# Attention in an encoder layer: row normalisation on VectorE, reciprocals for two rows at once, value tiles of two heads, the two output parts summed by a DMA, and another order of loads ahead of the up-projection

## The chip, the cores and the metric

The program runs on one core of one Trainium2 chip. A core has five engines with a queue each: TensorE (PE in the profile; its weight loads are PEld), VectorE (DVE), ScalarE (ACT), GpSimd (POOL) and SyncE (SP), which here only issues DMAs. Each engine works through its own queue in order and waits at semaphores for the others. The time is the device time of one execution in microseconds: before the change 1638.55 us, the median of three runs (1635.51 to 1639.82).

## The reference

One encoder layer on x of 1024 positions by 1024 channels, in float32 throughout. Cut to what matters here:

```python
h = layer_norm(x) * (1 + sc1) + sh1
proj = h @ w_in                    # q, k, v of 2 x 8 heads of 64, forget logits, two gates
# branch A, "fox": causal softmax attention, bias F[t] - F[s]
# branch B, "chunk": each block of 128 queries sees at most 5 key blocks, bias by distance
p = softmax(logits + bias)         # per head and query row
o = p @ v                          # 64 columns per head
merged = sigmoid(gate_a) * (o_a @ w_br_fox) + sigmoid(gate_c) * (o_c @ w_br_chunk)
x = layer_norm(alpha * x + (1 + g1) * (merged @ w_out), ln1_g, ln1_b)
u = causal_depthwise_conv(h2 @ w_up)                 # 1024 -> 2 x 2816
x = layer_norm(alpha * x + (1 + g2) * ((silu(a) * val) @ w_down), ln2_g, ln2_b)
```

## The kernel before

Every product is made of float32r operands that are split in a high part (a cast, on ACT) and a low part (the difference, on POOL or DVE), and summed as high*high + high*low + low*high. A weight that is loaded from memory passes `split` (L97 to L103): ACT casts `wh`, POOL subtracts `wl`; only then its buffer `ws` is free for the next load on SP. There are two `ws` buffers.

The attention loop (L678 to L717) takes eight pairs of heads, the chunk pairs 4 to 7 first, then the fox pairs 2, 3, 0, 1. Each head goes through four steps `g`; a step takes two blocks of 128 query rows, here called row 0 and row 1 of the step. While step n is finished, step n+1 is begun:

- `scores` (L429): two matmuls per piece of keys into `pss`, on DVE the bias and the row minimum (L460; `mx`), on ACT the exponential with the row sum `sm` (L466), on DVE its reciprocal `rc` (L468), and a multiplication of the row by `rc`: on ACT for row 0 if it has over 512 keys (L470), on POOL else (L472). In fox, POOL first prepares the diagonal piece of the bias, `fm` (L453).
- `probs` (L485): PE transposes the row in pieces of 128 keys (L501), ACT casts (L505), DVE subtracts (L506).
- `weighted` (L509): the transposed rows against the value tile `vs` of the head (L516). Its columns are the 64 high parts and the 64 low parts of the values, so the 128 rows of the result are two parts of the output that have to be added: ACT copies one half across (L520, `ot`), DVE adds (L521) into `o32`, a tile that two heads fill; one store to `od` per pair and half (L708).

Between these stand matmuls of the "stream" (projections of later heads, values, gates: L216 to L218, L312 to L314), which fill PE. A list scheduler puts the instructions of all engines in the order in which they are issued, by its own estimates, so a change at one place can move rows elsewhere.

After the attention come the branch products, the output product and the first normalisation, then the up-projection: for eight of the 22 blocks of columns (`c < HEAD`) in a form with prepared sums that `wd` holds, for the others from `w_up` directly. Blocks are taken in the order 0, 8, 1, 9, ... (L223). Weights wait in two buffers `fs` and two buffers `ws`. Of block 0, all four prepared parts are loaded early into `fs` (L992); `head` (L808) multiplies parts of blocks 0 to 7 ahead of the loop, with the two `ws`. The loop (L1146) lets the second half of a block alternate with the first half of the next; the eviction L1062 (`add`) reads a product that a later product of the block goes on summing in.

Of the kernel before, what the change touches and what calls it, by code (L numbers as in the profile page):

```python
# [11 lines left out]
F32 = mybir.dt.float32  # L12
# [6 lines left out]
P = 128  # L19
# [23 lines left out]
def body(ctx, tc, a, out):  # L43
# [256 lines left out]
    def unit_v(br, grp):  # L300
        n = 264 if (br, grp) == (1, 0) else 256

        def run(ws):
            tiles = [ap0.tile([P, NT, P], F32R, name=nm("vs"), tag="vs", bufs=6) for _ in range(4)]
            v_now[br, grp] = tiles
            for t in range(NT):
# [8 lines left out]
                for i in range(4):  # L315
                    src = ps[:, i * DH : (i + 1) * DH]
                    se.copy(out=tiles[i][:, t, 0:DH], in_=src)
                    ve.tensor_sub(out=tiles[i][:, t, DH:P], in0=src, in1=tiles[i][:, t, 0:DH])
# [110 lines left out]
    def scores(hd, g, i):  # L429
# [35 lines left out]
        sm = small.tile([P, 1], F32, name=nm("sm"), tag="sm")  # L465
        se.activation(out=st[:, 0:nk], in_=st[:, 0:nk], func=AF.Exp, scale=-1.0, bias=prev, accum_out=sm)  # L466
        rc = small.tile([P, 1], F32, name=nm("rc"), tag="rc")
        ve.reciprocal(out=rc, in_=sm)  # L468
        if nk > 512 and not i:
            se.mul(out=st[:, 0:nk], in_=st[:, 0:nk], mul=rc)  # L470
        else:
            po.tensor_scalar_mul(st[:, 0:nk], st[:, 0:nk], rc)  # L472
        return st
# [35 lines left out]
    def weighted(hd, g, which, pt, o32):  # L509
        br, h = hd[4], hd[5]  # L510
        vs = v_now[br, h // 4][h % 4]
        j0, nj = pv_span(br, g)
        ps = pso.tile([P, H], F32, name=nm("pso"), tag="o")
        for j in range(nj):
            for c in range(2):
                pe.matmul(ps[:, 0:256], vs[:, j0 + j, :], pt[c][j // 4][:, j % 4, :], start=j == 0 and c == 0,  # L516
                          stop=j == nj - 1 and c == 1)
        own, other = slice(which * DH, (which + 1) * DH), slice((1 - which) * DH, (2 - which) * DH)
        tmp = ap.tile([P, 256], F32, name=nm("ot"), tag="ot", bufs=1)
        se.copy(out=tmp[own, :], in_=ps[other, 0:256])  # L520
        ve.tensor_tensor(out=o32[own, g % 2 * 256 : (g % 2 + 1) * 256], in0=ps[own, 0:256], in1=tmp[own, :], op=ALU.add)  # L521
# [138 lines left out]
    o_now = {}  # L660
# [12 lines left out]
    sts = {(0, i): scores(heads[steps[0][:2]], 0, i) for i in range(2)}  # L673
# [4 lines left out]
    for u, (ip, _) in enumerate(plan):  # L678
# [5 lines left out]
        for n in range(8 * u, 8 * u + 8):  # L684
# [3 lines left out]
            for qt in range(2):  # L688
                if n + 1 < len(steps):
# [5 lines left out]
                    sts[n + 1, qt] = scores(heads[nip, ni], ng, qt)  # L695
                probs(hd, g, qt, sts.pop((n, qt)), pt)
                passed += 0.5 * cost_of(n)
                while stream.cur < upto and spent * main < passed * fill:
                    spent += stream.step()
                    ticks += 1  # L700
                    if ticks % 2 or next(beside, aside) is aside:
                        next(aside, None)
            if g % 2 == 0:
                if i == 0:
# [13 lines left out]
    for _ in chain(beside, aside):  # L718
        pass
# [645 lines left out]
```

## Time and profile before

| | before |
|---|---|
| median of three runs | 1638.55 us (1635.51 to 1639.82) |
| profiled execution, its own time | 1642.11 us |
| its span | 1640.3 us |
| PE busy | 1533.1 us (93%) |
| DVE, ACT, POOL busy | 1132.2, 819.2, 595.9 us |
| mean granted clock of PE | 0.977 |

Busy time is that in which an engine works; the matmuls overlap, so a busy PE is not PE at its peak. A wait in brackets behind an instruction is the time that the engine stood idle before it, with the writer that ended it. The median us from issue to landing of a DMA include its queueing.

### The profile page before, as it was taken

How to read it: one execution, taken by the hardware profiler on the slowest of the kernel's cores; microseconds unless marked ns; L12 is line 12 of the kernel's file. 1: busy time of each engine (PE TensorE's matmuls, PEld its weight loads, DVE VectorE, ACT ScalarE, POOL GpSimd, SP SyncE). 2: the span in 40 equal slices, each digit the busy share in tenths (PEclk: the TensorE clock that was granted, in tenths of full speed). 3: DMA queues.
4: the chain of work that ended last, by engine and by line, in shares of the span. 5: the costliest groups of instructions: out<-in, count | busy, mean ns of one | idle time of the engine just before them, and what ended most of it. 6: DMA issues, size and time to landing. Idle time of an engine off the chain costs nothing. (4 is left out here: it accounts for less than half of the span.)

```text
span 1640.3 us, 22725 instructions
## 1 busy us (share of the span) xinstructions
PE 1533.1 (93%) x7689; PEld 1280.5 (78%) x7689; DVE 1132.2 (69%) x2309; ACT 819.2 (50%) x1473; POOL 595.9 (36%) x579
## 2 busy tenths in 40 slices
PE   6898999989998999999898896999999999999996
PEld 3787788778887988887787675788888888888885
DVE  6738787687656555444759878477778776756688
ACT  3546555554554555664323536444454544456451
POOL 1124344343643454543106354544445454000000
PEclk9999999999999999999999897999999999999999
DMA  9035786776444133334644634533453222597552
GB/s 365 26 95 165 244 260 219 245 227 210 163 122 146 49 109 97 106 97 163 230 141 170 228 117 142 191 135 116 148 179 122 97 96 91 203 380 243 187 192 78
DMA packets 117957, 270.62 MB, mean 165 GB/s; under 512 B 12368, under 2 KB 21136, under 8 KB 117840
## 3 DMA queue, kind: packets, MB, share of 16 engines
q1 hardware_dynamic: 112560, 260.16, 47.9%
q10 hardware_dynamic: 4752, 7.17, 1.2%
q0 software_dynamic: 528, 1.84, 0.3%
q8 instruction: 61, 1.00, 0.2%
q14 instruction: 56, 0.46, 0.1%
HBM read 193.32 MB, written 67.40 MB: 159 GB/s over the span
## 5 line engine op out<-in xcount | busy, mean ns | idle before, releaser
L102 POOL TENSOR_TENSOR wl<-ws,wh 128x1024 fp32r<-128x1024 f32 x54 | 132.7, 2461 | 229.0 <-ACT wh L101 229.0
L472 POOL TENSOR_SCALAR s<-s,rc 128x128 f32<-128x128 f32 (+3 forms) x96 | 146.7, 1529 | 139.3 <-DVE rc L468 108.5
L792 PE MATMUL psu<-hc,wx 128*128 128x512 f32 x720 | 168.4, 389 | 0.0
L792 PEld LDWEIGHTS psu<-hc,wx 128*128 128x128 f32 x720 | 135.1, 188 | 28.1
L1030 DVE SCALAR_TENSOR_TENSOR pcv<-u,convp,pcv 128x1024 f32<-128x1024 f32 x88 | 113.2, 1286 | 45.6 <-ACT pcv L1028 44.6
L1171 DVE TENSOR_TENSOR op<-rw,op 128x512 fp32r<-128x512 f32 x146 | 93.5, 687 | 52.7 <-ACT op L1170 52.4
L466 ACT ACTIVATE s<-s,mx 128x640 f32<-128x640 f32 (+7 forms) x128 | 94.5, 739 | 69.3 <-DVE mx L460 68.2
L1170 ACT CAST op<-rw 128x512 fp32r<-128x512 f32 x146 | 85.2, 622 | 83.2 <-PE psd L1183 41.4
L505 ACT CAST pt<-pst 128x512 fp32r<-128x512 f32 (+1 forms) x192 | 82.0, 451 | 76.8 <-PE pst L501 73.3
L1182 PE MATMUL psd<-op,op 128*128 128x512 f32 x292 | 113.7, 389 | 0.9 <-DVE op L1171 0.9
L1181 PE MATMUL psd<-op,op 128*128 128x512 f32 x292 | 113.6, 389 | 0.0
L1183 PE MATMUL psd<-op,op 128*128 128x512 f32 x292 | 113.6, 389 | 0.0
L216 PE MATMUL psq<-h1h,wh 128*128 128x512 f32 x256 | 105.6, 414 | 0.0
L506 DVE TENSOR_TENSOR pt<-pst,pt 128x512 fp32r<-128x512 f32 (+1 forms) x192 | 96.4, 518 | 11.8 <-ACT pt L505 10.1
L216 PE MATMUL psg<-h1h,wh 128*128 128x512 f32 x256 | 103.9, 406 | 0.0
L217 PE MATMUL psq<-h1l,wh 128*128 128x512 f32 x256 | 102.1, 399 | 1.2 <-DVE h1l L213 1.2
L218 PE MATMUL psq<-h1h,wl 128*128 128x512 f32 x256 | 101.9, 398 | 0.8 <-POOL wl L102 0.8
L501 PE MATMUL pst<-ident,s 128*128 128x128 f32 x528 | 82.6, 276 | 19.5 <-POOL s L472 16.7
L218 PE MATMUL psg<-h1h,wl 128*128 128x512 f32 x256 | 100.2, 391 | 0.0
L217 PE MATMUL psg<-h1l,wh 128*128 128x512 f32 x256 | 100.1, 391 | 0.0
L516 PE MATMUL pso<-pt,vs 128*128 128x256 f32 x608 | 93.1, 291 | 3.6 <-DVE pt L506 3.1
L516 PEld LDWEIGHTS pso<-pt,vs 128*128 128x128 f32 x608 | 83.3, 194 | 12.7 <-DVE pt L506 4.9
(267 smaller groups left out, 4025.3 us busy)
## 6 DMA issues: line engine op xcount, KB each, us to landing
ws<-in_w_up SPq DMA_DIRECT2D x36, 512.0 KB, 3.4
wa<-in_w_ada SPq DMA_DIRECT2D x64, 256.0 KB, 3.4
dr<-in_w_down SPq DMA_DIRECT2D x22, 512.0 KB, 4.9
rw<-td SPq DMA_DIRECT2D x44, 256.0 KB, 4.6
yd<-y SPq DMA_DIRECT2D x20, 512.0 KB, 2.7
rw<-yd SPq DMA_DIRECT2D x40, 256.0 KB, 4.1
rw<-sd SPq DMA_DIRECT2D x33, 256.0 KB, 4.6
wa<-in_w_ada SPq DMA_DIRECT2D x8, 1024.0 KB, 10.7
```

The costliest lines, as they stand in the source:

```text
L102: po.tensor_sub(out=lo, in0=st, in1=hi)
L216: pe.matmul(ps, wh, xh, start=start, stop=False)
L217: pe.matmul(ps, wh, xl, start=False, stop=False)
L218: pe.matmul(ps, wl, xh, start=False, stop=stop)
L472: po.tensor_scalar_mul(st[:, 0:nk], st[:, 0:nk], rc)
L506: ve.tensor_sub(out=dl, in0=src, in1=dh)
L516: pe.matmul(ps[:, 0:256], vs[:, j0 + j, :], pt[c][j // 4][:, j % 4, :], start=j == 0 and c == 0, stop=j == nj - 1 and c == 1)
L792: pe.matmul(ps, w[:, a_, k, :], h[k][b_], start=first, stop=k == 3 and a_ == 1, skip_group_check=on)
L1030: ve.scalar_tensor_tensor(out=ps, in0=u[b][:, 2 - d : S + 2 - d], scalar=cp[:, 2 - d : 3 - d], in1=ps, op0=ALU.mult, op1=ALU.add)
L1181: pe.matmul(ps[t], g[:, 0, ts], d[:, 0], start=start, stop=False, skip_group_check=on)
L1182: pe.matmul(ps[t], g[:, 0, ts], d[:, 1], start=False, stop=False, skip_group_check=on)
L1183: pe.matmul(ps[t], g[:, 1, ts], d[:, 0], start=False, stop=stop, skip_group_check=on)
```

## The change

1. The sums of a step's two rows go into one tile of two columns; `normed` takes both reciprocals in one DVE instruction, after both exponentials, and multiplies each row: row 0 of over 512 keys on ACT as before, every other row on DVE. POOL has no part in it any more.
2. A value tile holds two heads (three buffers of two heads each in place of six of one), so the evictions of the values take two heads at a time: 64 casts and 64 subtractions in place of 128 each.
3. `weighted` ends with one ACT copy of all 128 rows into `o32`, which now belongs to one head; there is no addition on DVE. SP stores rows 0 to 63 of it to `od`; one step later POOL issues a DMA that adds rows 64 to 127 to the same place. That is 32 stores on SP in place of 16, and 32 DMAs on POOL.
4. Ahead of the up-projection, the two `fs` buffers take block 0's first two parts and the second half of the weights of block 8; block 0's other two parts go through `ws`.

```diff
...
-            tiles = [ap0.tile([P, NT, P], F32R, name=nm("vs"), tag="vs", bufs=6) for _ in range(4)]
+            tiles = [ap0.tile([P, 2, NT, P], F32R, name=nm("vs"), tag="vs", bufs=3) for _ in range(2)]
...
-                for i in range(4):
-                    src = ps[:, i * DH : (i + 1) * DH]
-                    se.copy(out=tiles[i][:, t, 0:DH], in_=src)
-                    ve.tensor_sub(out=tiles[i][:, t, DH:P], in0=src, in1=tiles[i][:, t, 0:DH])
+                for i in range(2):
+                    src = ps[:, i * P : (i + 1) * P].rearrange("p (h d) -> p h d", h=2)
+                    se.copy(out=tiles[i][:, :, t, 0:DH], in_=src)
+                    ve.tensor_sub(out=tiles[i][:, :, t, DH:P], in0=src, in1=tiles[i][:, :, t, 0:DH])
...
-        sm = small.tile([P, 1], F32, name=nm("sm"), tag="sm")
-        se.activation(out=st[:, 0:nk], in_=st[:, 0:nk], func=AF.Exp, scale=-1.0, bias=prev, accum_out=sm)
-        rc = small.tile([P, 1], F32, name=nm("rc"), tag="rc")
+        se.activation(out=st[:, 0:nk], in_=st[:, 0:nk], func=AF.Exp, scale=-1.0, bias=prev, accum_out=sm[:, i : i + 1])
+        return st[:, 0:nk]
+
+    def row_sums():
+        return small.tile([P, 2], F32, name=nm("sm"), tag="sm")
+
+    def normed(rows, sm):
+        rc = small.tile([P, 2], F32, name=nm("rc"), tag="rc")
         ve.reciprocal(out=rc, in_=sm)
-        if nk > 512 and not i:
-            se.mul(out=st[:, 0:nk], in_=st[:, 0:nk], mul=rc)
-        else:
-            po.tensor_scalar_mul(st[:, 0:nk], st[:, 0:nk], rc)
-        return st
+        for i, st in enumerate(rows):
+            if st.shape[1] > 512 and not i:
+                se.mul(out=st, in_=st, mul=rc[:, i : i + 1])
+            else:
+                ve.tensor_scalar_mul(st, st, rc[:, i : i + 1])
...
-        own, other = slice(which * DH, (which + 1) * DH), slice((1 - which) * DH, (2 - which) * DH)
-        tmp = ap.tile([P, 256], F32, name=nm("ot"), tag="ot", bufs=1)
-        se.copy(out=tmp[own, :], in_=ps[other, 0:256])
-        ve.tensor_tensor(out=o32[own, g % 2 * 256 : (g % 2 + 1) * 256], in0=ps[own, 0:256], in1=tmp[own, :], op=ALU.add)
+        se.copy(out=o32[:, g % 2 * 256 : (g % 2 + 1) * 256], in_=ps[:, 0:256])
...
-    sts = {(0, i): scores(heads[steps[0][:2]], 0, i) for i in range(2)}
+    sm = row_sums()
+    sts = {(0, i): scores(heads[steps[0][:2]], 0, i, sm) for i in range(2)}
+    normed([sts[0, i] for i in range(2)], sm)
+    owed = []
+
+    def added():
+        while owed:
+            to, o32 = owed.pop()
+            po.dma_start(out=to, in_=o32[DH:P, :], accum_op=ALU.add)
+
...
-                    sts[n + 1, qt] = scores(heads[nip, ni], ng, qt)
+                    if qt == 0:
+                        sm = row_sums()
+                    sts[n + 1, qt] = scores(heads[nip, ni], ng, qt, sm)
+                    if qt == 1:
+                        normed([sts[n + 1, i] for i in range(2)], sm)
...
+            added()
             if g % 2 == 0:
-                if i == 0:
-                    o_now[ip, g // 2] = ap.tile([P, H], F32, name=nm("o32"), tag="o32", bufs=2)
-            weighted(hd, g, i, pt, o_now[ip, g // 2])
-            if i == 1 and g % 2 == 1:
-                sy.dma_start(out=od[g // 2, ip], in_=o_now.pop((ip, g // 2)))
+                o_now = ap.tile([P, H], F32, name=nm("o32"), tag="o32", bufs=2)
+            weighted(hd, g, i, pt, o_now)
+            if g % 2 == 1:
+                to = od[g // 2, ip, i * DH : (i + 1) * DH, :]
+                sy.dma_start(out=to, in_=o_now[0:DH, :])
+                owed.append((to, o_now))
...
-    start = [summed(0, j, hbp, "fs") for j in (0, 2)]
+    start = summed(order[0], 0, hbp, "fs"), raw(order[1], 1, hbp, "fs")
...
-                self.w7, self.w3 = summed(c, 2, *((wp, "ws") if c != order[0] else (hbp, "fs")))
+                self.w7, self.w3 = summed(c, 2, wp, "ws")
...
```

How the order of instructions moves is shown at three places. First PE at the first fox head, step g = 1, from row 1's scores (`pss_4775`, after the change `pss_4538`) to the first transpose of row 0; `s_4726` (before) and `s_4493` (after) are row 0, `pso` the weighted sum of the step before, `pss_4806` and `pss_4811` (after: `pss_4569`, `pss_4574`) the scores of the next step's first row, `psq` a projection. Before:

```order
L446 MATMUL pss_4775<-qm_3995,qm_3757 128x512
L447 MATMUL pss_4775<-m_970_4379,qm_3757 128x512
L501 MATMUL pst_4789<-ident,s_4644 128x128 x2
L446 MATMUL pss_4806<-qm_3995,qm_3757 128x512
L447 MATMUL pss_4806<-m_970_4379,qm_3757 128x512
L501 MATMUL pst_4825<-ident,s_4726 128x128
L516 MATMUL pso_4795<-pt_1031_4724,vs_4183 128x256
L501 MATMUL pst_4825<-ident,s_4726 128x128 x2
```

After the change, from the two transposes right behind row 1's scores on, in two pieces that follow on each other:

```order
L506 MATMUL pst_4552<-ident,s_4416 128x128 x2
L446 MATMUL pss_4569<-qm_3816,qm_3586 128x512
L447 MATMUL pss_4569<-m_879_4173,qm_3586 128x512
L216 MATMUL psq_4516<-h1h_103,wh_4510 128x512
L521 MATMUL pso_4559<-pt_935_4490,vs_3996 128x256
L217 MATMUL psq_4516<-h1l_111,wh_4510 128x512
L521 MATMUL pso_4559<-pt_936_4491,vs_3996 128x256
L521 MATMUL pso_4559<-pt_935_4490,vs_3996 128x256
L521 MATMUL pso_4559<-pt_936_4491,vs_3996 128x256
L446 MATMUL pss_4574<-qm_3816,qm_3586 128x256
L447 MATMUL pss_4574<-m_879_4173,qm_3586 128x256
L218 MATMUL psq_4516<-h1h_103,wl_4511 128x512
```

```order
L216 MATMUL psq_4516<-h1h_104,wh_4510 128x512
L217 MATMUL psq_4516<-h1l_112,wh_4510 128x512
L218 MATMUL psq_4516<-h1h_104,wl_4511 128x512
L216 MATMUL psq_4516<-h1h_105,wh_4510 128x512
L217 MATMUL psq_4516<-h1l_113,wh_4510 128x512
L506 MATMUL pst_4584<-ident,s_4493 128x128 x3
```

Before, two transposes and two score matmuls stood between row 1's scores and the first transpose of row 0. After the change there are two transposes, four score matmuls (two of 256 columns), four weighted ones (of 256) and eight of the projection.

The same place on DVE (`sm_4736` is row 0's sum, `s_4774` row 1; after the change `s_4493` and `s_4537` are the two rows, `s_4568` is a row of the next step). Before:

```order
L468 RECIPROCAL rc_4738<-sm_4736 128x1
L540 TENSOR_TENSOR dr_8408<-dr_8408,dt_8476 128x512
L460 ISA s_4774,mx_4780<-pss_4775,fb_4382 128x384
L460 ISA mx_4780 128x1
L540 TENSOR_TENSOR dr_8408<-dr_8408 128x512
L460 ISA s_4774,mx_4782<-pss_4775,fm_4778,mx_4780 128x128
L460 ISA mx_4782 128x1
L506 TENSOR_TENSOR pt_1032_4725<-pst_4789,pt_1031_4724 128x2x128
L460 ISA s_4805,mx_4809<-pss_4806,fb_4382 128x512
L460 ISA mx_4809 128x1
```

After:

```order
L460 ISA s_4537,mx_4543<-pss_4538,fb_4176 128x384
L460 ISA mx_4543 128x1
L511 TENSOR_TENSOR pt_936_4491<-pst_4552,pt_935_4490 128x2x128
L460 ISA s_4537,mx_4545<-pss_4538,fm_4541,mx_4543 128x128
L460 ISA mx_4545 128x1
L460 ISA s_4568,mx_4572<-pss_4569,fb_4176 128x512
L460 ISA mx_4572 128x1
L460 ISA s_4568,mx_4579<-pss_4574,fm_4577,mx_4572 128x128
L460 ISA mx_4579 128x1
L473 RECIPROCAL rc_4548<-sm_4492 128x2
L478 TENSOR_SCALAR s_4493<-s_4493,rc_4548 128x384
L478 TENSOR_SCALAR s_4537<-s_4537,rc_4548 128x512
```

Row 0's reciprocal stood ahead of row 1's minima. Now one reciprocal for both stands behind row 1's minima and those of the next step's first row, with the two multiplications behind it.

Third, SP's loads ahead of the up-projection (`wd` is the prepared sums, `hf`, `p`, `u`, `s` are other operands). Before, in two pieces with three rows between them, of which none is a load into `ws`:

```order
L770 DMA ws_10804<-wd 128x2x512
L951 DMA hf_10732<-hx 128x512
L770 DMA ws_10806<-wd 128x2x512
L952 DMA hf_10733<-hx 128x512
L951 DMA hf_10768<-hx 128x512
L952 DMA hf_10769<-hx 128x512
L762 DMA ws_10949<-in_w_up 128x1024
L1076 DMA s_2511_11041<-in_w_up 128x512
```

```order
L1084 DMA p_2535_11203<-md 128x512
L762 DMA ws_11082<-in_w_up 128x1024
L770 DMA ws_11199<-wd 128x2x512
L762 DMA ws_11080<-in_w_up 128x1024
L770 DMA ws_11197<-wd 128x2x512
```

After, the same stretch in two pieces:

```order
L787 DMA ws_10412<-wd 128x2x512
L968 DMA hf_10340<-hx 128x512
L779 DMA ws_10414<-in_w_up 128x1024
L969 DMA hf_10341<-hx 128x512
L968 DMA hf_10376<-hx 128x512
L969 DMA hf_10377<-hx 128x512
L779 DMA ws_10557<-in_w_up 128x1024
L1093 DMA s_2328_10651<-in_w_up 128x512
```

```order
L1101 DMA p_2351_10811<-md 128x512
L787 DMA ws_10649<-wd 128x2x512
L779 DMA ws_10690<-in_w_up 128x1024
L787 DMA ws_10805<-wd 128x2x512
L1093 DMA s_2350_10809<-in_w_up 128x512
L787 DMA ws_10807<-wd 128x2x512
```

The second half of block 8's weights (`ws_11080` before, `ws_10414` after) moves from behind three other loads of weights to the place of block 0's second pair of sums; those (`ws_10649`) now come ahead of the first half of block 8 (`ws_10690`).

## Rows read from the trace of the kernel before

**Rows 1.** The page, its head and part 1: the span, then each engine's busy time, share of the span and number of instructions.

```profile
span 1640.3 us, 22725 instructions
...
PE 1533.1 (93%) x7689; PEld 1280.5 (78%) x7689; DVE 1132.2 (69%) x2309; ACT 819.2 (50%) x1473; POOL 595.9 (36%) x579
```

**Rows 2.** The view by stretches: start and end, length, then busy us (number of instructions) of PE, PEld, DVE, ACT and POOL, PE's mean granted clock (1.00 is 2.4 GHz), share of the DMA engines, GB/s. The first two stretches are the attention loop, the third is the turn into the up-projection, the last is the up-projection and most of the down-projection.

```profile
150.00:400.00 250.00, 229.29 (x1382) 200.99 (x1383) 192.62 (x502) 136.36 (x319) 102.13 (x141) 0.99 0.72 231
400.00:760.00 360.00, 348.13 (x2000) 301.53 (x1998) 202.83 (x619) 204.66 (x410) 169.02 (x201) 0.99 0.36 112
1000.00:1060.00 60.00, 44.42 (x176) 34.76 (x175) 37.77 (x44) 29.82 (x51) 33.67 (x28) 0.83 0.42 141
1060.00:1600.00 540.00, 539.12 (x2379) 446.09 (x2378) 394.71 (x498) 271.48 (x412) 167.43 (x129) 1.00 0.49 168
```

**Rows 3.** The view of waits of PE over the whole span: who waited, for which tile's writer, us in total, times, longest.

```profile
PE pst L501 <- POOL s L472: 16.7, 15, 2.8
PE pss L446 <- DVE mx L460: 11.5, 11, 3.4
PE psu L792 <- ACT wx L780: 3.6, 1, 3.6
```

**Rows 4.** The groups by line on POOL from 150 to 760 us: line, engine, operation, tiles, shapes, count | busy us, mean ns | idle before, and what ended it.

```profile
L472 POOL TENSOR_SCALAR s<-s,rc 128x384 f32<-128x384 f32 (+3 forms) x88 | 137.1, 1558 | 132.4 <-DVE rc L468 105.9 <-DVE vs L318 8.8 <-PE pso L516 8.1
L102 POOL TENSOR_TENSOR wl<-ws,wh 128x1024 fp32r<-128x1024 f32 x33 | 80.4, 2436 | 57.1 <-ACT wh L101 57.1
```

**Rows 5.** The groups by line and shape over the whole span, DVE and ACT; columns as in rows 4.

```profile
L468 DVE RECIPROCAL rc<-sm 128x1 f32<-128x1 f32 x128 | 20.4, 159 | 39.2 <-ACT s L466 38.1
...
L521 DVE TENSOR_TENSOR o<-pso,ot 64x256 f32<-64x256 f32 x64 | 26.9, 420 | 17.9 <-ACT ot L520 16.7
...
L318 DVE TENSOR_TENSOR vs<-psv,vs 128x64 fp32r<-128x64 f32 x128 | 28.2, 221 | 25.1 <-ACT vs L317 24.5
...
L421 DVE TENSOR_SCALAR cb<-cb 128x640 f32<-128x640 f32 x8 | 4.2, 528 | 2.6 <-DMA cb<-in_rel_t 2.6
...
L520 ACT COPY ot<-pso 64x256 f32<-64x256 f32 x64 | 23.4, 366 | 37.9 <-PE pso L516 36.9
...
L466 ACT ACTIVATE s<-s,mx 128x1024 f32<-128x1024 f32 x8 | 9.2, 1152 | 6.8 <-DVE mx L460 6.7
...
L470 ACT ACTIVATE s<-s,rc 128x896 f32<-128x896 f32 x8 | 8.3, 1044 | 0.3
```

**Rows 6.** The timeline of POOL and of DVE at 779 us: start, us, engine, line, operation, count.

```profile
779.46 2.34 POOL L102 TENSOR_TENSOR wl<-ws,wh 128x1024 fp32r<-128x1024 f32 x1 [3.54 <-ACT wh L101]
...
779.69 2.20 DVE L198 TENSOR_SCALAR gc<-ones,modc 128x128 f32<-128x128 f32 x1
...
782.41 0.47 DVE L198 TENSOR_SCALAR gc<-ones,modc 128x128 f32<-128x128 f32 x2
```

**Rows 7.** The timeline of the attention loop at 415 to 422 us: the third query block of the first forgetting head (the score tile of 384 keys is row 0 of its step, the one of 512 is row 1).

```profile
415.34 2.41 POOL L102 TENSOR_TENSOR wl<-ws,wh 128x1024 fp32r<-128x1024 f32 x1
...
416.18 2.12 DVE L540 TENSOR_TENSOR dt<-dr,dr 128x512 f32<-128x512 f32 x1 [0.39 <-DMA dr<-in_w_down]
...
418.44 0.40 PE L447 MATMUL pss<-m,qm 128*128 128x512 f32 x1
...
418.60 1.68 POOL L472 TENSOR_SCALAR s<-s,rc 128x384 f32<-128x384 f32 x1
...
420.33 0.33 PE L501 MATMUL pst<-ident,s 128*128 128x128 f32 x1 [1.50 <-POOL s L472]
...
422.09 0.19 ACT L466 ACTIVATION_READ_ACCUMULATOR s<-s,mx 128x1 f32 x1
```

**Rows 8.** The timeline at the start of the up-projection, SP's loads first, then DVE, then PE.

```profile
1025.81 0.33 SPq L762 DMA_DIRECT2D ws<-in_w_up  x1
...
1033.26 0.33 SPq L762 DMA_DIRECT2D ws<-in_w_up  x1
...
1037.69 0.76 DVE L1100 TENSOR_TENSOR s<-ws 128x512 f32<-128x512 f32 x1 [4.68 <-DMA ws<-in_w_up]
...
1042.51 1.75 DVE L778 TENSOR_TENSOR wt<-ws,ws 128x512 f32<-128x512 f32 x1
...
1044.19 1.28 DVE L1062 TENSOR_TENSOR u<-psu,p 128x512 f32<-128x512 f32 x2
...
1030.41 2.88 PE L792 MATMUL psu<-ha,wh 128*128 128x512 f32 x12
...
1045.01 4.58 PE L792 MATMUL psu<-hc,wh 128*128 128x512 f32 x12 [3.56 <-ACT wx L780]
```

**Rows 9.** The view by stretches for the four us in which PE goes on after that wait; columns as in rows 2.

```profile
1045.00:1049.00 4.00, 3.99 (x11) 3.17 (x12) 0.46 (x1) 0.00 (x0) 2.85 (x3) 0.57 0.00 0
```

**Rows 10.** The DMA issues by line (KB each, median us from issue to landing), then POOL's time to issue one, and the last pair's attention output on DVE and on SP.

```profile
od<-o SPq DMA_DIRECT2D x16, 256.0 KB, 4.2
...
sd<-sc POOLq DMA_DIRECT2D x3, 256.0 KB, 3.8
...
1427.10 0.54 POOL L1057 DMA_DIRECT2D sd<-sc  x1 [0.20 <-issue]
...
703.73 0.42 DVE L521 TENSOR_TENSOR o<-pso,ot 64x256 f32<-64x256 f32 x1 [1.18 <-ACT ot L520]
...
750.48 0.38 SPq L708 DMA_DIRECT2D od<-o  x1
```

More of the change, by code (lines that the diff above doesn't have):

```diff
@@ L427, in first_block, with scores @@
         return 0 if br == 0 else max(0, qi - 4)
-    def scores(hd, g, i):
+    def scores(hd, g, i, sm):
         q, m1, m2, bias, br, h = hd
@@ L510, in weighted @@
         br, h = hd[4], hd[5]
-        vs = v_now[br, h // 4][h % 4]
+        vs = v_now[br, h // 4][h % 4 // 2]
         j0, nj = pv_span(br, g)
@@ L515, in weighted @@
             for c in range(2):
-                pe.matmul(ps[:, 0:256], vs[:, j0 + j, :], pt[c][j // 4][:, j % 4, :], start=j == 0 and c == 0,
+                pe.matmul(ps[:, 0:256], vs[:, h % 2, j0 + j, :], pt[c][j // 4][:, j % 4, :], start=j == 0 and c == 0,
                           stop=j == nj - 1 and c == 1)
-        own, other = slice(which * DH, (which + 1) * DH), slice((1 - which) * DH, (2 - which) * DH)
-        tmp = ap.tile([P, 256], F32, name=nm("ot"), tag="ot", bufs=1)
-        se.copy(out=tmp[own, :], in_=ps[other, 0:256])
-        ve.tensor_tensor(out=o32[own, g % 2 * 256 : (g % 2 + 1) * 256], in0=ps[own, 0:256], in1=tmp[own, :], op=ALU.add)
+        se.copy(out=o32[:, g % 2 * 256 : (g % 2 + 1) * 256], in_=ps[:, 0:256])
     def mod(v, half):
@@ L659, in body @@
     heads = {}
-    o_now = {}
     def ensure(n):
@@ L717, in body @@
         qk.pop(ip)
+    added()
     for _ in chain(beside, aside):
@@ L1057, in stored @@
             eng.dma_start(out=sd[i, j], in_=x)
-    raws.update({(0, 0): start[0], (0, 2): start[1]})
+    raws.update({(order[0], 0): start[0], (order[1], 1): start[1]})
     def add(out, x, y):
```

## The prediction

> **What bounds the kernel now.** The page comes first: PE is busy for 1533.1 of 1640.3 us, so at most 107 us of idle time can be won, and DVE, ACT and POOL have slack on the mean [rows 1]. The view by stretches shows where that idle time lies: in the attention loop PE works 229.29 of 250 and 348.13 of 360 us, in the turn into the up-projection 44.42 of 60, and from there to 1600 us 539.12 of 540 [rows 2]. The change touches the attention loop, where PE stands 32.6 us, and the turn, where it stands 15.6. Behind it nothing can be won.
>
> Next the waits of PE, by the tile waited for [rows 3]. Three lines belong to the change: the transposes wait for POOL's multiplication 15 times, 16.7 us in all; the score matmuls wait for DVE's minima 11 times, 11.5 us; and one matmul of the up-projection waits 3.6 us for a cast of weights. A bound on the gain is thus 31.8 us, plus what the clock gives back.
>
> **The base.** The profiled execution took 1642.11 us, 1.8 more than its span. The median of the three runs is 3.56 us lower. Durations are from the profiled execution, and I take the difference off the median.
>
> **Loads ahead of the up-projection.** The timeline of this place is read backwards from PE [rows 8]. The last twelve matmuls ahead of the wait start at 1030.41; the next can only start at 1045.01, after 3.56 us, when ACT's cast is there. DVE is what is late: it waits 4.68 us for a load until 1037.69, and behind that instruction stand the subtractions L778 (one at 1042.51, 1.75 us) and the eviction L1062 at 1044.19. That load was issued by SP only at 1033.26, 7.45 us behind the one at 1025.81, for it needs a buffer that POOL had to free first. With the new order this part (the second half of block 8) comes three weight loads earlier into an `fs` buffer, which waits for nobody. Then DVE is past L1100 before PE comes to ask: the 3.56 us go. What follows the wait goes too: the twelve matmuls behind it take 4.58 us where the same twelve took 2.88 ahead of it [rows 8], at a granted clock of 0.57, that is at nearly the lower of the two levels, 1.2 GHz [rows 9]. That is 4.58 - 2.88 = 1.70 us. Sum: -5.3. The step pays with block 0's second pair of sums, which now goes through `ws` ahead of block 8's first half and pushes that back by one load. The loads of this place follow each other at 3.7 us (7.45 for two of them, one load lies between the rows), so the other end is -5.3 + 3.7 + 3.6 = +2, if the wait only changes places. Range -5.3 to +2; I take -5.3, because PE has the other parts of block 0 to work on meanwhile.
>
> **Normalisation off POOL.** POOL loses 137.1 us in 88 multiplications of 1.56 us in the loop [rows 4]. DVE gets 96 (six per head, those after the prologue's included). Per head the widths sum to 128+384+256+512+768+1024 = 3072 keys in fox and 2560 in chunk, 45,000 in sixteen heads; at 0.528 us for 640 columns of the same operation [rows 5] that is 37 us. DVE loses the 64 additions L521 (26.9), 64 of 128 reciprocals (64 x 0.159 = 10.2), and, of 28.2 us of value subtractions, between nothing and 14.1; I take 10 [rows 5]. Net 37 - 26.9 - 10.2 - 10 = -10 us on DVE, 3% of its 395 us in the loop [rows 2]. The busy time decides nothing; the order does.
>
> The typical wait is in the timeline at 418 us [rows 7]. Row 1's last score matmul ends at 418.84. POOL takes from 418.60 to 420.28 for row 0, and PE's first transpose of row 0 starts at 420.33 after 1.50 us idle. After the change row 0 has to wait for row 1's exponential as well, whose accumulator is read at 422.28, 3.44 us after row 1's scores; then the reciprocal for both, 0.16 [rows 5], and 384 columns of multiplication, 0.32: 3.92 us. The order gives PE work for part of that. Between row 1's scores and row 0's transpose stand ten matmuls of 512 columns, six of 256 and two transposes; by 2.88/12 = 0.24 us each, halves by halves [rows 8], this is 2.4 + 0.72 + 0.1 = 3.2 us. PE waits 3.92 - 3.2 = 0.7 us in place of 1.50. Sixteen heads have this step: 11.2 us. In the last fox pair, where no projection is left to put between, the wide rows of 1024 (exponential 1.152, and ACT's multiplication of 896, 1.044 [rows 5]) make the chain some 0.6 us longer than the cover; six such steps make 3.5 us, an estimate. 11.2 + 3.5 = 14.7 in place of 16.7: -2.0.
>
> Bounds of this term. Below: all 16.7 us go, and a third of the 11.5 for the minima, since POOL no longer works beside DVE for 137 us: -20. Above: DVE's multiplications are held up by POOL as the next rival prices it: +15. I take -2, the value that the row at hand gives, and -1 of the 11.5 for the DVE time saved (3%, and fewer instructions beside POOL).
>
> **The rest** I cost at nothing. ACT's copy is the same instruction with 128 rows in place of 64; it is 0.366 us [rows 5]. The 64 fewer casts on ACT and subtractions on DVE are hidden behind the stream. The 32 stores and 32 adding DMAs lie beside the loop, where the DMA engines are busy 0.72 and 0.36 of the time [rows 2]; POOL's issue takes 0.54 us, its 256 KB land in 3.8, SP's in 4.2 [rows 10]. The cover is POOL's free time; if that is gone, the third rival holds.
>
> Forecast: -5.3 - 2.0 - 1.0 = -8.3; 1638.55 - 8.3 = 1630 us. Its own range is 1623 to 1635.
>
> **Rivals.** *All the waits go* (0.20). If the scheduler's cover is longer than I count in most steps, POOL's 16.7 vanish with a third of the waits for minima: 1638.55 - 5.3 - 20 = 1613. For it: DVE's multiplication costs a third of POOL's 1.56. Against it: row 0 now ends later than before.
>
> *DVE is held up by POOL* (0.12), the slower side. The trace has the same operation of DVE at 2.20 us beside a POOL subtraction of two inputs from 779.46 to 781.80, and at 0.235 when it is alone [rows 6]; another of DVE, two inputs, took 2.12 beside the same kind of POOL instruction [rows 7]. Both end as POOL's ends, or just behind. In the loop POOL runs that line for 80.4 us [rows 4] of 610, 13%. A multiplication that starts beside one waits half of its 2.44 on the mean: 96 x 0.13 x 1.22 = 15 us, on a DVE that works in order, and for a row that PE waits for. If all of it reaches PE and the 16.7 us stay as waits for DVE, it is 1638.55 - 5.3 + 15 = 1648. It decides once more than about 10 of the 15 us reach PE. Against it: transposes are often ready long before, with 15 waits in 64 steps.
>
> The Trainium skill, "SBUF — State Buffer", section "Who interferes with whom", has it as a rule: DVE in a two-port mode, which a multiplication by a scalar can enter, and GpSimd take a shared port pair for a whole instruction, and the second is blocked until the first ends. By that rule the additions L521 (PSUM and SBUF) were free of it and their successors are not, which speaks against this change and would draw the time from 1630 towards this rival's 1648; the 2.20 and 0.235 us of [rows 6] agree with it.
>
> *POOL stands behind its adding DMA* (0.06). It waits until SP's store has landed. The last pair's sum was ready at 704.1 and SP issued its store at 750.48, 46 us later [rows 10]. The adding DMA is one step behind, 610/64 = 9.5 us; so POOL would stand 37 us, with a subtraction of weights behind it. One is needed each 610/33 = 18 us, and two buffers cover one of them: 37 - 18 = 19 us late, 1638.55 - 5.3 + 19 = 1652. Against it: that lag is at the end of the loop, where fewer loads follow.
>
> *Nothing comes of it* (0.17). The attention waits only change their name, 16.7 for POOL to about as much for DVE, and the up-projection's wait moves to the delayed half of block 8: 1638.
>
> **How the numbers follow.** The forecast has 0.45. A difference of 0.3%, 4.9 us, is about what can be told from none: faster is below 1633.6, slower above 1643.5. Faster: all of the first rival, 0.38 of the forecast's 0.45 and 0.02 of the last: 0.60. Slower: both slow rivals and 0.02 of the last: 0.20. The remaining 0.20 is the same. The range 1612 to 1648 leaves out the lower part of the first rival (0.08), half of the DVE rival (0.05) and the adding DMA (0.06).
>
> **What would show it.** In the waits of PE: no wait of `psu` for `wx` at the start of the up-projection, and the twelve matmuls there at 0.24 us each; `pst` waiting for `s` from DVE and no longer from POOL, 12 to 17 us in sum, most of them in step 1 of a head. In the groups: DVE's multiplications near 0.39 us on the mean; over 0.5 speaks for the DVE rival. On POOL: no adding DMA behind a wait of over 10 us. The forecast is wrong if PE's waits for DVE's rows go beyond 20 us or vanish, or if the turn keeps a wait of 3 us or more.

## The result and the profile after

The changed kernel is slower: 1643.88 us, the median of 20 runs (1634.20 to 1653.45), against 1638.66 for 20 runs of the kernel before (1633.76 to 1643.82). The ratio is 1.0033, its 95% interval 1.0018 to 1.0049. The forecast was 1630. The profiled execution of the changed kernel took 1641.76 us, 2.1 less than the median; where small costs count, the ratios of runs decide below, and the traces tell where to look.

The page, its head and part 1, which answers to [rows 1]:

```profile
span 1639.0 us, 22509 instructions
...
PE 1536.2 (94%) x7689; PEld 1279.2 (78%) x7689; DVE 1139.7 (70%) x2213; ACT 809.5 (49%) x1409; POOL 483.6 (30%) x515
```

POOL has lost 112 us; DVE has not lost 10 but gained 7.5. The stretches of [rows 2], same columns:

```profile
150.00:400.00 250.00, 233.89 (x1450) 207.56 (x1450) 191.47 (x471) 136.75 (x306) 57.15 (x117) 0.99 0.79 241
400.00:760.00 360.00, 344.12 (x1915) 293.43 (x1913) 203.03 (x558) 195.16 (x373) 107.26 (x164) 0.98 0.39 114
1000.00:1060.00 60.00, 46.42 (x193) 36.67 (x192) 42.11 (x46) 31.01 (x52) 36.55 (x29) 0.86 0.43 146
1060.00:1600.00 540.00, 539.12 (x2378) 446.14 (x2378) 394.16 (x498) 272.15 (x413) 166.84 (x128) 1.00 0.48 168
```

In the first part of the attention loop PE works 4.6 us more than before, in the second 4.0 us less. The waits of PE that answer to [rows 3]:

```profile
PE pss L446 <- DVE mx L460: 9.1, 8, 3.5
PE pst L506 <- DVE s L478: 8.1, 4, 2.6
PE pst L506 <- ACT s L476: 6.1, 6, 2.0
...
PE psu L809 <- ACT wx L797: 1.5, 1, 1.5
```

The rows are still waited for, 8.1 + 6.1 = 14.2 us in place of 16.7. The sum is close to the 14.7 of the prediction, but not its parts: two of the four waits for DVE, 2.6 us each, are of another kind. They lie in the last pair of heads. The timeline of the first (start, us, engine, line, operation, tiles, shapes, count, idle time before it):

```profile
672.90 0.46 POOL L453 TENSOR_TENSOR fm<-fb,cmask 128x128 f32<-128x128 f32 x1
...
673.28 0.47 SPq L723 DMA_DIRECT2D od<-o  x1
...
678.00 0.84 POOL L682 DMA_DIRECT2D od<-o  x1 [4.64 <-DMA od<-o]
678.60 0.73 POOL L453 TENSOR_TENSOR fm<-fb,cmask 128x128 f32<-128x128 f32 x1
...
679.36 0.35 DVE L460 CUSTOM_DVE_ANT_0 s<-pss,fm,mx 128x128 f32<-128x128 f32 x1 [2.84 <-POOL fm L453]
...
679.83 1.04 DVE L478 TENSOR_SCALAR s<-s,rc 128x384 f32<-128x384 f32 x2
...
680.52 0.55 PE L506 MATMUL pst<-ident,s 128*128 128x128 f32 x3 [2.61 <-DVE s L478]
```

SP issues the store of the first half at 673.28. POOL stands 4.64 us at its adding DMA until that store has landed, and behind the DMA stands `fm`, the diagonal piece of the bias for the next step. DVE works in order: it stands for `fm` with the two multiplications behind it, and PE stands for row 0. The view of waits puts this down to DVE's multiplication; the DMA is three steps back in the timeline.

### The profile page after: what moved, and what is told of

Same layout as the page of the kernel before. It is cut to its first block, busy times and chain, and to the rows that moved or that the text cites. A ratio compares the mean times of both kernels' runs of the same rounds, so it can differ in the third digit from the quotient of the medians.

```text
span 1639.0 us, 22509 instructions
## 1 busy us (share of the span) xinstructions
PE 1536.2 (94%) x7689; PEld 1279.2 (78%) x7689; DVE 1139.7 (70%) x2213; ACT 809.5 (49%) x1409; POOL 483.6 (30%) x515
## 5 line engine op out<-in xcount | busy, mean ns | idle before, releaser
L101 ACT CAST wh<-ws 128x1024 fp32r<-128x1024 f32 x54 | 56.3, 1049 | 67.6 <-PE psq L217 22.6
```

## The experiments

All ratios are to the kernel before, run beside it. The change, e1 to e4, e5 to e8, e9 to e12, e13 to e16, and e17 with e18 ran on six occasions, so a difference such as that from e6 to e17 is one of two ratios. Differences of two ratios below have their two half intervals added in squares.

| | what runs | ratio, interval | median us |
|---|---|---|---|
| after | the change | 1.0033, 1.0018 to 1.0049 | 1643.9 |
| e1 | part 4 (loads) alone | 0.9984, 0.9973 to 0.9995 | 1634.8 |
| e2 | parts 1 to 3 | 1.0045, 1.0025 to 1.0065 | 1643.4 |
| e3 | the change without part 1 | 1.0066, 1.0050 to 1.0082 | 1648.8 |
| e4 | the change without part 3 | 0.9925, 0.9909 to 0.9940 | 1625.7 |
| e5 | adding DMA held back on POOL | 1.0017, 1.0005 to 1.0030 | 1640.8 |
| e6 | POOL writes, adds nothing | 0.9986, 0.9973 to 1.0000 | 1635.0 |
| e7 | part 1 alone | 0.9955, 0.9939 to 0.9971 | 1630.1 |
| e8 | e4, reciprocal per row | 0.9912, 0.9898 to 0.9926 | 1622.4 |
| e9 | SP writes both halves | 0.9930, 0.9907 to 0.9952 | 1627.6 |
| e10 | e4 and 32 writes by POOL | 0.9922, 0.9903 to 0.9941 | 1627.2 |
| e11 | e4 and 32 adding DMAs | 0.9971, 0.9954 to 0.9988 | 1634.8 |
| e12 | e8, halves added when loaded | 0.9943, 0.9925 to 0.9961 | 1631.1 |
| e13 | the change, no DMA on POOL | 0.9946, 0.9929 to 0.9964 | 1630.4 |
| e14 | e6, held back on POOL | 0.9977, 0.9958 to 0.9997 | 1633.8 |
| e15 | e9 and 32 writes by POOL | 0.9945, 0.9925 to 0.9965 | 1631.1 |
| e16 | e9 and the adding DMA | 1.0015, 0.9995 to 1.0035 | 1642.7 |
| e17 | POOL adds without waiting | 1.0013, 0.9998 to 1.0029 | 1640.4 |
| e18 | part 2 (value tiles) alone | 0.9976, 0.9957 to 0.9996 | 1634.5 |

**Which part costs.** e1 is the diff of part 4 alone, e2 all but that, e3 and e4 take a part back.

> The kernel before with part 4 (the order of loads ahead of the up-projection) alone. Common to all theories, from the two profiles: from the last normalisation matmul to the end the changed kernel is 3.4 us ahead of the kernel before (1.99 us late at the first psu matmul, 1.39 us early at the last psd matmul), so this run should be 3 to 4 us faster: ratio 0.998. If it is not faster, the 3.4 us were the chance of one execution each.

> Parts 1 to 3 (the attention) without part 4. Result so far: the changed kernel is slower by 1.0033, some 5.4 us, while its profiled execution is 0.3 us shorter. If the loads are worth -3.4 us, the attention costs +8.8 us: ratio 1.0053. Theory A (rows normalised in pairs on DVE come late) and theory B (the adding DMA on POOL) expect the same here; the theory that the loads are the loss expects 1.000 or below.

> The changed kernel with part 1 undone: each row has its own reciprocal again and is multiplied on POOL (row 0 of over 512 keys on ACT); the adding DMA, the value tiles of two heads and the loads stay. Theory A: the loss goes, ratio 0.996 to 0.999, PE waits again for POOL's rows, about 16 us. Theory B: the loss stays, ratio 1.003 or more, because POOL now has multiplications and adding DMAs in one queue.

> The changed kernel with part 3 undone: ACT copies one half across, DVE adds, SP stores 256 KB for both heads; no adding DMA. The rest stays. Theory B: the loss goes, ratio 0.996 to 0.999, and the times spread as narrowly as those of the kernel before. Theory A: the loss stays, ratio 1.003 to 1.005 (DVE has 27 us more to do).

The loads gain 0.16% (e1). Without part 1 the loss grows (e3), so the pairing and DVE's multiplications are not the loss: theory A falls. Without part 3 the loss turns into a gain of 0.75% (e4). From e4 to the changed kernel it is 1.08% (0.86 to 1.30), some 17.7 us, which part 3 costs. In e4 the waits for rows are nearly gone, and the first line is that for the minima:

```profile
PE pss L446 <- DVE mx L460: 16.4, 11, 4.4
...
PE pst L506 <- ACT s L476: 0.6, 1, 0.6
```

**The other parts alone.** e7 is part 1 on the kernel before, e18 part 2. In e8 a row is normalised when its own exponential is done:

```diff
-            po.tensor_scalar_mul(st[:, 0:nk], st[:, 0:nk], rc)
+            ve.tensor_scalar_mul(st[:, 0:nk], st[:, 0:nk], rc)
```

> The kernel before with part 1 alone: one reciprocal for both rows, multiplications on DVE (ACT for wide row 0); no other part. From e4 against e1: parts 1 and 2 together are worth 0.9925 - 0.9984 = -0.6%, some 9.7 us. The prediction had -3 us for part 1 (ratio 0.998). If part 1 carries the whole: 0.994. If the value tiles carry it: 0.999 to 1.000. By the rival of the prediction (DVE held up by POOL) it would be 1.005.

> The kernel before with part 2 (value tiles of two heads) alone, the one part that has not run by itself: e4 is 0.9925, norm (e7) times loads (e1) is 0.9955 x 0.9984 = 0.9939, so the value tiles are left with 0.9986, about -2 us. The prediction had them in the DVE saving, -1 us in all: 0.999 to 1.000.

> e4 (all but the adding DMA) with a reciprocal for each row, right behind its own exponential, and the multiplication on DVE where e4 has it: pairing of the rows is undone, POOL stays free. If taking the multiplication off POOL is what counts: as e4, 0.992 to 0.994. If the pair (64 reciprocals fewer, another order) counts: 0.996 or more. If the pair costs, because row 0 waits for row 1: below 0.991.

Part 1 is worth 0.45%, part 2 0.24%. With part 4 they multiply to 0.9915, and e4, which has all three, is at 0.9925. e8 is the fastest of all and ahead of both kernels: 1622.4 us. Between it and e4 lie 0.13% (-0.08 to 0.34), so what pairing the reciprocals costs, if it does, isn't told from nothing, and part 1's gain is there without it.

**The wait or the DMA.** e5 holds the adding DMA back on POOL by two things: it is issued a step later, and behind the newest `fm` or zeroing (`po_last`).

```diff
-            added()
+            added(n - 2)
...
+            with tc.issue_after(po_last[0]):
+                po.dma_start(out=to, in_=o32[DH:P, :], accum_op=ALU.add)
```

e6 keeps the 32 DMAs and takes away the adding (`oe` is a place of its own); e17 adds, but all 32 times to one small place that nobody else writes or reads; e13 issues nothing; e14 is e6 held back as in e5.

```diff
-            po.dma_start(out=to, in_=o32[DH:P, :], accum_op=ALU.add)
+            po.dma_start(out=to, in_=o32[DH:P, :])                    # e6: to in oe
+            po.dma_start(out=oe, in_=o32[DH:P, :], accum_op=ALU.add)  # e17
```

> The changed kernel with each adding DMA held back on POOL alone, behind the preparation of the diagonal bias (fm) or the zeroing of the probability tiles of the next step; the order on PE, DVE, ACT and the work itself are the same. Measured so far: the changed kernel is at 1.0033, without the adding DMA (e4) at 0.9925, so the adding DMA costs 1.1%, some 18 us. Theory W (POOL stands until SP's store has landed, and what stands behind the DMA on POOL, fm above all, comes late): most of it comes back, ratio 0.993 to 0.996; the two waits of 2.6 us of PE in the last pair go. Theory D (the DMA itself costs: its 0.84 us of POOL, its traffic, its reads of memory): nothing comes back, ratio 1.002 to 1.004.

> The changed kernel with POOL's 32 DMAs kept but as plain writes of the second half into a place of their own: they add nothing and wait for no store of SP's (the sum of the two halves is left out). Theory W: ratio 0.992 to 0.995, POOL's wait for od of 56 us gone. Theory D: the 32 DMAs of POOL stay, ratio 1.002 to 1.004. If adding in memory is what costs, and not the wait, it is also 0.992 to 0.995 here, but e5 then stays at 1.003.

> e6 with POOL's 32 DMAs adding again, but into one small place that is zeroed at the start and that SP never writes and nobody reads: adding without the wait for SP's store (the sum of the halves is left out). PE, DVE, ACT and SP in the order of e6 and of the changed kernel. If the wait for the store (and for the last landing behind the loop) is what e6 took away: as e6, 0.997 to 1.000. If the adding itself is dear, wherever it goes: as the changed kernel and e5, 1.001 to 1.004.

> The changed kernel without POOL's DMA: the second half of the attention output is stored nowhere (the sum of the halves is left out). PE, DVE, ACT and SP have the order of e6 to the last instruction; e6 is this plus 32 writes by POOL, the changed kernel this plus 32 adding ones. So far: e6 0.9986, e9 (same work, SP writes, DVE and SP in another order) 0.993. Theory P (the DMAs of POOL cost, in this order): 0.992 to 0.995. Theory O (the order of DVE, ACT and SP that came with part 3 costs): 0.997 to 1.000, as e6.

> e6 with POOL's plain writes held back on POOL as in e5, behind the next step's fm or zeroing; other engines in the same order. If what e6 keeps is POOL standing for ACT's copy (16.9 us in its profile) ahead of urgent work: 0.993 to 0.996. If it is the order of the other engines, or the DMA itself wherever it stands: 0.997 to 1.000.

These five have the order of the changed kernel on PE, DVE, ACT and SP but for at most 11 instructions of an engine, so they make a ladder. No DMA on POOL: 0.9946. 32 plain writes: 0.9986, or 0.9977 where they are held back. 32 adding ones without a wait: 1.0013. Adding ones with the wait: 1.0033, or 1.0017 held back. One thing more moves: at 19 of the 32 places the DMA of e6 and e17 stands one to three instructions earlier in POOL's queue than that of the changed kernel. In e5 DVE's wait for `fm` is gone, and POOL's wait for the store falls from 56.3 us (the changed kernel) to 15.1 (e5; who waited, for which tile's writer, us, times, longest):

```profile
POOL od L682 <- DMA od<-o: 56.3, 17, 6.2
```

```profile
POOL od L685 <- DMA od<-o: 15.1, 4, 5.9
```

For that e5 gains 0.16% (-0.04 to 0.36). So theory W holds for what the timeline showed, and falls as the cause of the whole. From no DMA to adding ones that wait for no store it is 0.67% (0.44 to 0.90), and the wait adds 0.20% (-0.02 to 0.42), which isn't told from nothing; the two waits of PE in the profiled execution are 5.2 us. Two pairs differ in the adding and keep POOL's order as well: e6 to e17 with 0.27% (0.06 to 0.48), and e14 to e5, both held back, with 0.40% (0.17 to 0.63; at one place of 32 the order differs, and e5 still waits 15.1 us for stores). Between e6 and e14 lie 0.09% (-0.15 to 0.33): that plain writes cost by standing for ACT's copy is not borne out.

**The DMA or the order.** Part 3 also changes the order on all engines. e9 lets SP write the second half; e10 and e11 put DMAs on POOL into e4; e15 and e16 put them into e9; e12 does without adding in the loop.

```diff
-            po.dma_start(out=to, in_=o32[DH:P, :])
+            sy.dma_start(out=to, in_=o32[DH:P, :])                    # e9, beside e6
```

> e6 with the second half written by SP in place of POOL: the same 64 writes of 128 KB, no adding, nothing on POOL (the sum of the halves is left out). So far: e4 (ACT and DVE add, one write of 256 KB) 0.9925, e6 0.9986, the changed kernel 1.0033. Theory P (a DMA that POOL issues costs by itself, about 6 us of the 10 that e6 keeps): ratio near 0.993. Theory O (the loss that e6 keeps is in the order and the buffers that come with part 3, whoever writes): it stays at 0.997 to 1.000.

> e4, in which no DMA adds, with 32 more DMAs of 128 KB on POOL that write the finished sums a second time to a place nobody reads; the order on PE, DVE, ACT and SP is that of e4 to the last instruction. Theory P: 0.9925 rises to about 0.998. Theory O: it stays within 0.991 to 0.995, since POOL is idle most of the time.

> e4 with POOL adding the finished sums once more to where SP has just stored them (32 adding DMAs of 128 KB that wait for SP's store; the attention output is doubled), the order on PE, ACT and SP almost that of e4. Over e10 it has the wait and the adding. If the wait and the adding cost what e6 gave back (0.5%): 0.5% above e10. If the adding DMA is costly only in the order that part 3 brings: as e10.

> e9, where SP writes both halves, and POOL writes the second half once more to a third place, nothing adds: PE, DVE, ACT and SP in the order of e9 to the last instruction (the sum of the halves is left out). Theory P: up from 0.993 to about 0.998. Theory O: stays at 0.991 to 0.995.

> e9's order with the adding DMA of the changed kernel: SP writes the first half to its place and the second to a spare one, POOL adds the second half to the first half's place, and the output is whole. Adding and its wait cost 0.47% in the order of the changed kernel (e6) and 0.49% in that of e4 (e11). Theory O: 0.993 + 0.005 = 0.998, 0.5% below the changed kernel. Theory P: POOL's DMAs cost their 0.56% here too: 1.002 to 1.004.

> A version that adds nothing in the loop and nothing by DMA: e8 (one reciprocal per row, multiplications on DVE), but ACT copies both halves as in the changed kernel, SP stores both in places of their own, and DVE adds them when they are loaded for the branch products. It saves DVE 64 additions of 0.42 us in the loop and pays eight of 1024 columns and eight more loads behind it. Theory P: 0.989 to 0.992, as e8 or better. Theory O (the order and buffers of part 3 are the loss): 0.996 or more.

Without a DMA on POOL the three orders lie together: e13 0.9946, e9 0.9930, e4 0.9925. Theory O falls as the cause of the whole. Plain writes on POOL cost 0.40% in the order of the changed kernel, 0.15% in that of e9 and nothing (-0.03%) in that of e4, each give or take 0.2 to 0.3: small, and not the same everywhere; theory P in its first form falls too. e10 and e15 came out as theory O had them, e9 and e13 as theory P, and e6, e12 and e16 lie between the ranges that were set for them, so no theory had the whole. What costs in every order is adding in place of writing, the wait and the other place in POOL's queue included (19 of 32 places from e15 to e16 too, 27 from e10 to e11): 0.47% (e6 to the change), 0.70% (e15 to e16), 0.49% (e10 to e11). e12 gains 0.57%, but is 0.31% (0.08 to 0.54) behind e8: with ACT copying both halves and the additions behind the loop the kernel is slower than with the additions in it.

**What an adding DMA does to others.** In the changed kernel it holds POOL for 0.84 us, where the plain one of e6 holds it for 0.55, and it lands after 3.6 us in place of 3.2. In one pair of traces the loads beside it land later. DMA issues (KB each, median us from issue to landing) in e13, and then in e17:

```profile
dr<-in_w_down SPq DMA_DIRECT2D x22, 512.0 KB, 3.9
m<-qm SPq DMA_DIRECT2D x32, 256.0 KB, 4.3
```

```profile
dr<-in_w_down SPq DMA_DIRECT2D x22, 512.0 KB, 4.3
m<-qm SPq DMA_DIRECT2D x32, 256.0 KB, 5.4
...
oe<-o POOLq DMA_DIRECT2D x32, 128.0 KB, 4.5
```

These are 0.4 and 1.1 us more, but adding doesn't account for them. The same two loads in the changed kernel, which adds as well:

```profile
dr<-in_w_down SPq DMA_DIRECT2D x22, 512.0 KB, 4.0
m<-qm SPq DMA_DIRECT2D x32, 256.0 KB, 4.5
```

In e6, where POOL only writes, they land after 4.3 and 4.8 us, and in the kernel before after 4.9 and 5.0. PE's idle time in the loop does grow along the ladder, one trace each. The view by stretches, columns as in [rows 2], in e13 and then in e17:

```profile
150.00:760.00 610.00, 583.76 (x3414) 506.45 (x3413) 396.88 (x1035) 336.86 (x683) 147.21 (x254) 0.99 0.53 164
```

```profile
150.00:760.00 610.00, 576.78 (x3363) 499.35 (x3363) 396.14 (x1025) 332.71 (x675) 169.24 (x283) 0.99 0.56 166
```

PE stands 26.2 and 33.2 us; in e6 it is 28.9 and in the changed kernel 32.0. Aligned matmul by matmul, e17 is 3.6 us ahead of e13 at 200 us and 7.4 behind it at 600, in pieces of up to 2 us, a few of them gains. One such place, in e13 and then in e17, where DVE stands for a load (`wa`), multiplies two rows, and POOL subtracts weights:

```profile
485.28 0.75 DVE L152 SCALAR_TENSOR_TENSOR acc<-wa,cond,acc 128x512 f32<-128x512 f32 x1 [1.40 <-DMA wa<-in_w_ada]
485.95 2.72 DVE L478 TENSOR_SCALAR s<-s,rc 128x128 f32<-128x128 f32 x2
...
486.12 2.40 POOL L102 TENSOR_TENSOR wl<-ws,wh 128x1024 fp32r<-128x1024 f32 x1 [2.59 <-ACT wh L101]
...
487.24 0.27 PE L506 MATMUL pst<-ident,s 128*128 128x128 f32 x1
```

```profile
488.92 0.75 DVE L156 SCALAR_TENSOR_TENSOR acc<-wa,cond,acc 128x512 f32<-128x512 f32 x1 [1.65 <-DMA wa<-in_w_ada]
489.59 3.17 DVE L482 TENSOR_SCALAR s<-s,rc 128x128 f32<-128x128 f32 x2
...
489.60 2.37 POOL L106 TENSOR_TENSOR wl<-ws,wh 128x1024 fp32r<-128x1024 f32 x1 [2.67 <-ACT wh L105]
...
492.77 0.30 PE L510 MATMUL pst<-ident,s 128*128 128x128 f32 x1 [1.89 <-DVE s L482]
```

The two rows of a count of x2 are row 0 (128 keys) and row 1 (256). In e13 DVE starts 0.17 us ahead of POOL, row 0 is done at 486.23 after 0.28 us, and only row 1 is held, until 488.67. In e17 DVE waited 0.25 us longer for its load, both start within 0.01 us, and row 0 itself is held until 492.62: PE stands 1.89 us. This is how a load that lands a quarter of a microsecond later costs two. But it doesn't show what adding costs, for no adding DMA was under way here. The two nearest in e17:

```profile
466.93 0.83 POOL L686 DMA_DIRECT2D oe<-o  x1 [1.24 <-ACT o L527]
...
492.49 0.83 POOL L686 DMA_DIRECT2D oe<-o  x1
```

The slowest of the 32 landed after 6.6 us. Nor are such places more frequent with adding: of the 96 multiplications two took over 1.4 us in e13, two in e17 and one in the changed kernel, and all 96 take 51.3, 52.7 and 49.1 us. That the adding DMA costs is shown by the runs; by what way it takes its time from PE stays open.

## Why the prediction was wrong

**The step that failed** is the sentence "The rest I cost at nothing", with the 32 adding DMAs that "lie beside the loop" under the cover of POOL's free time. POOL was free, as assumed (57 and 107 us busy in 250 and 360 us). But that is busy time. What stands behind a DMA in POOL's queue was not asked for (`fm`), nor what adding costs over writing. Part 3, put at nothing, measured +17.7 us (e4 to the change), and it alone turns the sign: without it the same kernel gains 12.3 us (e4: 0.0075 x 1639), more than the 8.3 forecast. POOL's DMA is 14 us of the 17.7 (e13 to the change: 0.87%, 0.64 to 1.10); the rest, 0.21% from e4 to e13, isn't told from nothing. None of the signs that the prediction set for being wrong came: PE waits 8.1 us for DVE's rows, neither over 20 nor none, and 1.5 at the turn. They watched the terms of the sum, and the loss lay in what was left out of it.

**The third rival** had the mechanism, POOL standing for SP's store, at a chance of 0.06, but the wrong place and size. The lag of 46 us between sum and store was misread from [rows 10]: the addition at 703.73 is the first of the four that fill the tile stored at 750.48. The last is

```profile
749.39 0.43 DVE L521 TENSOR_TENSOR o<-pso,ot 64x256 f32<-64x256 f32 x1 [4.44 <-ACT ot L520]
```

so the store followed 0.66 us behind it. In the changed kernel POOL issued its DMA 2.8 to 5.2 us after SP's store, 32 times. What was late was `fm`, not a weight, and the wait is worth some 3 us of the 17.7 (0.16 to 0.20%, with intervals from nothing to 7 us).

**The loads** were to bring -5.3 and brought -2.6 (e1, -0.8 to -4.4). The place in the changed kernel, SP, DVE and PE, which answers to [rows 8]:

```profile
1031.99 0.33 SPq L779 DMA_DIRECT2D ws<-in_w_up  x1
...
1036.82 1.75 DVE L1119 TENSOR_TENSOR s<-s,ws 128x512 f32<-128x512 f32 x1 [2.44 <-DMA ws<-in_w_up]
...
1041.01 1.77 DVE L795 TENSOR_TENSOR wt<-ws,s 128x512 f32<-128x512 f32 x1 [1.83 <-POOL wx L798]
...
1045.22 2.98 PE L809 MATMUL psu<-hc,wh 128*128 128x512 f32 x12 [1.49 <-ACT wx L797]
```

The wait is 1.49 in place of 3.56 us, since DVE now stands for the load that was pushed back. The other half of the term was right: the twelve matmuls behind the wait take 2.98 us, not 4.58, and the granted clock stays at 1.00, which answers to [rows 9]:

```profile
1044.00:1048.00 4.00, 2.78 (x12) 2.36 (x13) 1.67 (x3) 0.62 (x2) 4.00 (x3) 1.00 0.02 4
```

**Part 1** was sized at -3 and is worth -7.4 (e7). The step that failed is the product of 0.7 us and sixteen heads. At the place that it was worked out for it came near; the first fox head at step 1 in the changed kernel (PE, ACT, DVE, DVE, PE):

```profile
407.91 0.39 PE L447 MATMUL pss<-m,qm 128*128 128x512 f32 x1
...
410.32 0.18 ACT L465 ACTIVATION_READ_ACCUMULATOR s<-s,mx 128x1 f32 x1
...
410.95 0.35 DVE L460 CUSTOM_DVE_ANT_0 s<-pss,fm,mx 128x128 f32<-128x128 f32 x1 [0.68 <-POOL fm L453]
...
411.22 0.16 DVE L473 RECIPROCAL rc<-sm 128x2 f32<-128x2 f32 x1
...
412.12 0.55 PE L506 MATMUL pst<-ident,s 128*128 128x128 f32 x3 [0.46 <-DVE s L478]
```

From the end of row 1's last score matmul (408.30) to PE's transpose it is 3.82 us, where 3.92 were forecast, and PE waits 0.46, not 0.7. But the parts are others, so this is luck. To the end of row 1's exponential (410.50) it takes 2.2 us, not 3.44; then DVE stands 0.68 us for `fm`, which is late behind the adding DMA. The 3.44 us were misread from [rows 7]: the matmul at 418.44 belongs to the next step's first row, as the order of instructions shows. Row 1's own last one, before the change, and what its exponential stood behind on ACT:

```profile
417.75 0.39 PE L447 MATMUL pss<-m,qm 128*128 128x512 f32 x1
...
421.09 0.48 ACT L505 CAST pt<-pst 128x384 fp32r<-128x384 f32 x1 [2.32 <-PE pst L501]
...
421.46 0.73 ACT L466 ACTIVATE s<-s,mx 128x512 f32<-128x512 f32 x1
```

From 418.14 to 422.28 it took 4.14 us. Row 1's minima were there at 420.52, but ACT stood until 421.09 for the transposes of row 0, which had waited for POOL, and the exponential came behind their cast. This wait goes with the change.

Nor does the wait come back in sixteen heads: PE waits for DVE's rows four times in all: here, twice behind the adding DMA, and once for rows behind a DVE instruction of 2.73 us beside POOL (214 us). The 6.1 us for ACT's rows lie at six places all over the loop, not in the last pair, where the prediction had 3.5. That 14.2 is near 14.7 is luck too. With part 1 alone (e7) there are two:

```profile
PE pst L506 <- DVE s L478: 3.8, 2, 2.6
```

In e4 the waits for rows are 0.6 us in all: nearly everywhere PE has enough to do ahead of the rows. That is the first rival's premise, for which I had 0.20. Its other half failed: the waits for the minima were to fall by a third and rose from 11.5 to 16.4 us in e4.

**The multiplications** on DVE, in the changed kernel (groups by shape, columns as in [rows 5]):

```profile
L318 DVE TENSOR_TENSOR vs<-psv,vs 128x128 fp32r<-128x128 f32 x64 | 18.4, 288 | 24.2 <-ACT vs L317 24.0
...
L478 DVE TENSOR_SCALAR s<-s,rc 128x640 f32<-128x640 f32 x16 | 8.9, 553 | 0.3
...
L478 DVE TENSOR_SCALAR s<-s,rc 128x128 f32<-128x128 f32 x16 | 6.3, 392 | 0.2
```

640 columns take 0.553 us (0.528 was used), but 128 take 0.392 where proportion gives 0.11: a cost for each instruction, and the ones held beside POOL. All 96 sum to 49.1 us, not 37, a mean of 0.51 us. That is past the 0.5 at which the prediction would have its second rival speak, yet at the shortest time of each width they would still be 43.4. The values take 18.4 in place of 28.2, the saving of 10 as forecast. The second rival's mechanism is real (the held rows above took 2.5 and 3.0 us, the free one 0.28), and its price was not 15 us: part 1, with its 96 multiplications on DVE, is faster by itself (e7). The Trainium skill, "SBUF — State Buffer", section "Who interferes with whom", says that of GpSimd and a DVE instruction in a two-port mode whichever issues first has the shared ports for its whole instruction, and the other is blocked. The place from e13 agrees, where 0.17 us of lead let row 0 through; in e17, with 0.01 us between them, the trace cannot tell who was first.

**Value tiles**, hidden behind the stream in the forecast, gain 3.9 us alone (e18, 0.7 to 7.0).

## What to carry to other kernels

A DMA that an engine issues stands in that engine's queue with its wait: ask which store it waits for, how long that takes to land, and what the next instruction behind it is, however idle the engine looks. A small change of several parts is run part by part before it is believed: here three gains of 0.16 to 0.45% were covered by one loss of 1.08%. And a chain read from one place of a timeline is checked against the order of instructions, so that it starts at the right one, and against other places before it is multiplied by sixteen.

## What was not expected of the hardware

A DMA that adds to memory cost the kernel 0.47 to 0.70% more than one that writes the same 128 KB, in three orders of the program (its wait and its place in POOL's queue included). Where it waited for nobody's store it was 0.27% (0.06 to 0.48, e6 to e17), with PE, DVE, ACT and SP doing the same work in almost the same order and POOL in the same; where both were held back it was 0.40% (0.17 to 0.63, e14 to e5). It held POOL for 0.84 us at a time (1.03 in e11, 0.55 for a plain write) and landed after 3.6 to 4.7 us (3.2 to 3.4).
